# Forming weight sums and differences in a prologue by adding transfers instead of by VectorE

## The chip, the cores and the metric

The kernel runs on one core of a Trainium2 chip. The metric is the time of one execution on the device in microseconds (us); lower is better. Where several runs are given, the median counts.

## What is computed

One hybrid decoder layer on x (1024 positions x 1024 channels, float32):

```python
h = rmsnorm(x, pre_g)
proj = h @ w_in                  # 9248 columns: z, xBC, dt, q, k, v, f, z_att, g_ssm, g_att
A = ssd(silu(conv(xBC)), softplus(dt + dt_bias)) ...   # gated, group-normed
B = forgetting_attention(q, k, v, log_sigmoid(f + fgate_b)) * silu(z_att)
merged = sigmoid(g_ssm) * (A @ w_branch_ssm) + sigmoid(g_att) * (B @ w_branch_att)
out = x + rmsnorm(merged @ w_out, post_g)
```

Only the beginning matters here: h, its transpose, the first columns of h @ w_in, and dt and f (32 columns).

## The kernel before, in words

**Products with seven multiplications.** Every large product W^T h runs over blocks of 2 x 2. The weights are taken in pairs of 128 columns; one pair is four blocks a11, a12, a21, a22 (each 128 x 4 x 128, 256 KB; first digit the column group, second the half of the 1024 inputs). The transposed h is four blocks b11, b12, b21, b22 (each four tiles of 128 x 512). Instead of eight block products, seven are made, of sums of weight blocks with differences of h blocks:

- weights: S1 = a21 + a22, S2 = S1 + a11, S2 + a12, and a11 + a21
- h: T1 = b12 - b11, T2 = b22 - T1, T3 = T2 - b11, T4 = T2 - b21
- products, by the numbers that the code uses: 1 (a11, b11), 2 (a12, b21), 6 (S2, -T2), 5 (S1, T1), 7 (a11 + a21, T3), 4 (a22, T4), 3 (S2 + a12, -b22)

Each operand is kept in two parts of less precision, `h` (high) and `l` (the rest); `split` (lines 345 to 351) makes those of the weights (`wop`) with one ScalarE copy and one VectorE subtraction, `put` (line 1211) those of h (`x0h`, `x0l` for b11; x1 b21; x2 -b22; x3 T1; x4 -T2; x5 T3; x6 T4). One product ("step") is 12 matmuls of 128 x 512 on TensorE, issued as two halves of six. The results of a pair are collected in PSUM tiles `pb`, `pc`, `pd`.

**Order of the work.** `Pair` holds a pair of weight column groups; `prepare` (line 358) forms its sums and splits; `USES` (line 326) says which steps must be prepared before a raw weight buffer is free again, which is what `load_more` (line 510) goes by; raw weights have six buffers, sums two. `Stream` holds all pairs in a row and a written-out list of steps, and interleaves the first three pairs p, q, r: p1, q1, p2, q2, p6, p5, p7, p4, p3, q6, q5, q7, r1, q4, q3, then r2 and so on. `half` issues half a step; when a step begins, `ahead` (line 597) prepares the step three further on. So all the work beside the products is put between halves of steps. A scheduler then orders the instructions of each engine; `pin` keeps an instruction in its written place among the pinned ones, `tc.issue_after` puts one behind another. Each engine, and each queue that issues transfers (SyncE = SP, ScalarE = ACT, GpSimd = POOL), works strictly in its own order.

**The prologue** (from line 1166). x is loaded in eight tiles of 128 rows and normalised: tiles 0 to 3 by VectorE (line 1201), tiles 4 to 7 by GpSimd (line 1203). The first loop (k = 0 to 7) transposes tiles 0 to 3 on TensorE into PSUM (`pt`), copies them scaled to `low` (b11 and b21), splits them, and issues the halves of p1 and q1. Then `w_out` is copied within the device memory (`wo_dram`, 12 transfers of 256 KB on SyncE, line 1237), for use at the kernel's end. The second loop (j = 0 to 3, lines 1240 to 1263) transposes tiles 4 to 7: ScalarE copies the two transposed tiles out of PSUM to `up` (b12) and `b` (b22); four small products with 32 weight columns (`df`) give dt and f; VectorE forms T1 and T2 from `up`, `b`, and `low`, which are split; one half of p2 or q2 is issued; VectorE forms T3 and T4 in place of `low`. What is called the tail below are lines 1264 to 1280 and what stands right behind them: T3, T4 and -b22 are split while p6, p5, p7 and p4 run, and `dft`, with `summing`, brings dt and f into columns.

Then come convolution and state-space scan beside the further pairs, attention beside the late ones, and the final products; these the change doesn't touch.

## Time and profile before

| what | value |
|---|---|
| median of 3 runs | 1277.86 us (1277.46 to 1280.73) |
| the profiled execution's own time | 1273.87 us |
| its span, first to last instruction | 1272.2 us |
| mean granted TensorE clock | 0.999 |
| TensorE busy | 1246.1 us (98%) |
| VectorE busy | 1012.9 us (80%) |
| ScalarE busy | 794.3 us (62%) |
| GpSimd busy | 319.3 us (25%) |
| moved by transfers | 233.56 MB, 184 GB/s over the span |

How to read the profile: PE is TensorE's matrix multiply, PEld its weight load, DVE VectorE, ACT ScalarE, POOL GpSimd, SP SyncE; with a q behind it (SPq) an engine's issuing of transfers. L1203 is line 1203 of the kernel. A timeline row has start and length in us from the span's start, engine, line, operation, output <- inputs, size, and in brackets the idle time before it with what ended it; "x4" merges four such instructions in a row. A group's row has the count, the busy time in us and the mean length in ns, then the idle time before its instructions. A row of the windows view has the stretch, its length, the busy us of PE, PEld, DVE, ACT and POOL with the number of instructions, the granted clock, the busy share of the transfer engines, and GB/s.

### The profile page before, as it was taken

To read this page: it belongs to the slowest core of one execution; us is meant where nothing else is said; L and a number is where in the kernel's file an instruction comes from. 1 tells how busy PE (TensorE), PEld (TensorE's weight loads), DVE (VectorE), ACT (ScalarE), POOL (GpSimd) and SP (SyncE) were. 2 spreads that over 40 slices of the span, in tenths; PEclk is the share of its full clock that TensorE was granted. 3 is DMA by queue.
4 is the path that set the end of the run, shared out by engine and by line. 5 is a ranking of instruction groups with operands and counts; after the bars stand their busy time and mean duration, and the time that the engine had idled before them with its cause. 6 is when DMAs were issued, how large, how long until landed. Compare 5 with 4: busy or idle time off the path is not lost.

```text
span 1272.2 us, 20822 instructions
## 1 busy us (share of the span) xinstructions
PE 1246.1 (98%) x6926; PEld 982.3 (77%) x6926; DVE 1012.9 (80%) x1994; ACT 794.3 (62%) x1737; POOL 319.3 (25%) x322
## 2 busy tenths in 40 slices
PE   5999999999999999999999999999999999999997
PEld 3678888888888888888887777777777777778886
DVE  7988886988888978997767676767789767886975
ACT  7745665556665765566555666666687666844753
POOL 4000440013400241115102124223112212356062
PEclk9999999999999999999999999999999999999999
DMA  8232452545436533744447576666687657766933
GB/s 300 69 120 76 146 162 88 191 152 182 138 101 215 175 127 117 219 146 140 142 149 252 162 228 212 217 214 218 232 286 263 224 184 249 249 221 199 364 110 105
DMA packets 152236, 233.56 MB, mean 184 GB/s; under 512 B 15201, under 2 KB 60737, under 8 KB 152129
## 3 DMA queue, kind: packets, MB, share of 16 engines
q1 hardware_dynamic: 136064, 196.08, 47.7%
q10 hardware_dynamic: 10560, 18.06, 3.8%
q0 software_dynamic: 5504, 18.09, 3.7%
q8 instruction: 54, 0.88, 0.3%
q14 instruction: 54, 0.43, 0.1%
HBM read 162.99 MB, written 72.34 MB: 185 GB/s over the span
## 4 chain that ended last, share of the span: by engine, by line
PE 86%; DMA 4%; DVE 4%; ACT 4%; issue 1%; SPq 0%; POOL 0%; DVEq 0%; ACTq 0%; POOLq 0%
PE pb L128 36%; PE pc L128 21%; PE pd L128 7%; PE av L128 5%; PE pt L131 5%; PE s L128 5%; PE yps L128 2%; PE st L128 1%; ACT ex L1509 1%; DMA xt<-in_x 1%; PE tr L131 1%; PE tr_v L131 1%; DMA v<-v_dram 1%; PE df L128 1%; DVE wop L350 1%
## 5 line engine op out<-in xcount | busy, mean ns | idle before, releaser
L350 DVE TENSOR_TENSOR wop<-sum,wop 128x512 fp32r<-128x512 f32 x180 | 140.2, 780 | 53.6 <-ACT wop L349 52.6
L349 ACT ACTIVATE wop<-sum 128x512 fp32r<-128x512 f32 x180 | 112.5, 626 | 109.0 <-DVE sum L355 52.4
L1509 ACT ACTIVATE ex<-ex,nm 128x512 f32<-128x512 f32 (+1 forms) x192 | 116.2, 606 | 71.9 <-DVE nm L1505 71.6
L402 ACT ACTIVATE s<-pb 128x512 f32<-128x512 f32 x144 | 85.3, 593 | 98.2 <-PE pb L128 96.2
L128 PE MATMUL pb<-x0h,wop 128*128 128x512 f32 x384 | 131.5, 399 | 0.0
L128 PE MATMUL pb<-x6h,wop 128*128 128x512 f32 x384 | 129.5, 395 | 1.3 <-ACT s L402 1.3
L128 PE MATMUL pb<-x5h,wop 128*128 128x512 f32 x384 | 130.1, 396 | 0.7 <-ACT s L402 0.7
L350 DVE TENSOR_TENSOR wop<-raw,wop 128x512 fp32r<-128x512 f32 x144 | 105.4, 733 | 31.8 <-ACT wop L349 31.5
L128 PE MATMUL pc<-x3h,wop 128*128 128x512 f32 x384 | 129.8, 396 | 0.5 <-DVE ot L419 0.4
L128 PE MATMUL pc<-x2h,wop 128*128 128x512 f32 x384 | 130.2, 397 | 0.0
L128 PE MATMUL pb<-x4h,wop 128*128 128x512 f32 x384 | 129.1, 395 | 0.0
L1505 DVE CUSTOM_DVE_ANT_0 ex<-s,fb 128x512 f32<-128x512 f32 (+1 forms) x192 | 96.8, 552 | 20.0 <-PE s L128 14.8
L349 ACT ACTIVATE wop<-raw 128x512 fp32r<-128x512 f32 x144 | 89.7, 623 | 14.7 <-PE pd L128 6.1
L128 PE MATMUL pd<-x1h,wop 128*128 128x512 f32 x288 | 96.3, 394 | 0.0
L128 PEld LDWEIGHTS pb<-x6h,wop 128*128 128x128 f32 x384 | 72.1, 188 | 18.6 <-issue 2.0
L128 PEld LDWEIGHTS pb<-x5h,wop 128*128 128x128 f32 x384 | 72.1, 188 | 18.4 <-issue 2.0
L128 PEld LDWEIGHTS pb<-x0h,wop 128*128 128x128 f32 x384 | 72.6, 189 | 17.6 <-issue 2.9
L128 PEld LDWEIGHTS pc<-x3h,wop 128*128 128x128 f32 x384 | 72.1, 188 | 17.7 <-issue 1.5
L128 PEld LDWEIGHTS pc<-x2h,wop 128*128 128x128 f32 x384 | 72.1, 188 | 17.4 <-issue 2.4
L128 PEld LDWEIGHTS pb<-x4h,wop 128*128 128x128 f32 x384 | 72.1, 188 | 16.7 <-issue 1.9
L211 POOL TENSOR_TENSOR wd<-wd 128x256 f32<-128x256 f32 x32 | 32.4, 1011 | 205.0 <-DMA wd<-in_wo 135.0
L131 PE MATMUL pt<-ident,ex 128*128 128x128 f32 x576 | 75.1, 273 | 2.0 <-ACT ex L1509 1.4
(318 smaller groups left out, 2993.6 us busy)
## 6 DMA issues: line engine op xcount, KB each, us to landing
raw<-in_wu SPq DMA_DIRECT2D x128, 256.0 KB
csb<-cs_dram SPq DMA_DIRECT2D x32, 256.0 KB
q<-q_dram SPq DMA_DIRECT2D x32, 256.0 KB
k<-k_dram SPq DMA_DIRECT2D x16, 512.0 KB
fb<-f_dram SPq DMA_DIRECT2D x16, 512.0 KB
rb<-st_dram SPq DMA_DIRECT2D x48, 128.0 KB
wd<-in_wo SPq DMA_DIRECT2D x40, 128.0 KB
xt<-in_x SPq DMA_DIRECT2D x8, 512.0 KB
```

What stands on the lines that cost most here:

```text
L128: return tc.keep_in_program_order(nc.tensor.matmul(*args, **kw))
L131: return tc.keep_in_program_order(nc.tensor.transpose(out_, in_, idn))
L211: pin(nc.gpsimd.tensor_tensor(t[out_], t[a_], t[b_], ALU.subtract))
L349: nc.scalar.activation(op[:, 0], src, AF.Copy)
L350: nc.vector.tensor_tensor(op[:, 1], src, op[:, 0], ALU.subtract)
L402: nc.scalar.activation(s, ps, AF.Copy)
L1505: nc.vector.tensor_tensor_reduce(o, s[e][:, 0:w], fb[hp, h][:, e, 0:w], 1.0, 3.0e38, ALU.add, ALU.min, nm)
L1509: pin(nc.scalar.activation(o, o, AF.Exp, scale=-1.0, bias=nm, accum_out=hd.at(hd.sm, i, h, e)))
```

## The change

1. **Weight sums by transfers that add.** The first pair is gathered "fully", the next two "partly". `gather` loads a21 from device memory into a `sum` tile on SyncE and lets GpSimd issue a transfer that adds a22 to it: that is S1. For the first pair a second tile gets a21, then a22 and a11 added, S2. The raw a21 gets a11 added by a transfer, and S2 gets a12 added by one. For q and r S2 itself is still formed by VectorE. `FEWER` takes the place of `USES` for these pairs.
2. **When it happens.** The first pair is gathered behind the normalisation of tiles 4 to 7; each next one when step 5 of the pair before it is prepared. `ahead` prepares p6 and p5 together when p2 begins (before: p6 at the start of q1, p5 at that of p2).
3. **T1 and T2 out of PSUM.** `low` is kept negated. T1 is one VectorE instruction from the transposed tile in PSUM and `low`, T2 likewise from the other transposed tile and T1. `up` is not copied; `b22` is. The `df` products take -b11, -b21, T1 and b22, and `dft` and `summing` are adapted (signs, one more small copy).
4. **T3 and T4 by transfers that add.** T2 is added to `low` by GpSimd transfers within the on-chip memory, seven of eight; T3 of the last turn stays on VectorE. T2 has two buffers of its own.
5. **The copies of w_out** stand behind the last split of the prologue, ahead of its last five halves.

```diff
         USES = {"a11": (1, 6, 7), "a12": (2, 6), "a21": (6, 7), "a22": (6, 4)}
+        FEWER = {"a11": (1, 6), "a12": (2,), "a21": (7,), "a22": (4,)}
...
+            if self.gathers and self.s1 is not None and "a21" in names:
+                self.add(self.raw["a21"], "a11")
...
+        def add(self, t, n):
+            with tc.issue_after(self.behind) if self.behind else nullcontext():
+                nc.gpsimd.dma_start(t, self.source(n), accum_op=ALU.add)
+
+        def gather(self):
+
+            for n in range(2 if self.gathers == "fully" else 1):
+                t = wp.tile([P, KH, P], F32, tag="sum", bufs=2, name="sum")
+                nc.sync.dma_start(t, self.source("a21"))
+                self.add(t, "a22")
+                if n == 0:
+                    self.s1 = t
+                else:
+                    self.add(t, "a11")
+                    self.s2 = t
+            if "a21" in self.raw:
+                self.add(self.raw["a21"], "a11")
...
             elif which == 6:
-                self.s2 = self.total(self.s1, r["a11"])
+                if self.gathers != "fully":
+                    self.s2 = self.total(self.s1, r["a11"])
                 self.split(6, self.s2)
+                if self.gathers:
+                    self.add(self.s2, "a12")
+                    return
...
+            elif which == 7 and self.gathers:
+                self.split(7, r["a21"])
...
+            p.gathers, q.gathers, r.gathers = "fully", "partly", "partly"
...
             p.prepare(which)
+            following = self.pairs[self.pairs.index(p) + 1 :][:1]
+            if which == 5 and following and following[0].gathers:
+                following[0].gather()
             self.load_more()
...
-            if self.at + 3 < len(self.steps):
-                p, which = self.steps[self.at + 3]
+            for n in {1: (), 2: (4, 5)}.get(self.at, (self.at + 3,)):
+                if n >= len(self.steps):
+                    return
+                p, which = self.steps[n]
...
-                nc.scalar.activation(low[:, k, :], pt, AF.Copy, scale=preg[:, k : k + 1])
+                nc.scalar.activation(low[:, k, :], pt, AF.Copy, scale=less[:, k : k + 1])
...
         norm_tiles(1, tiles2)
-
-        for k, h in [(k, h) for j in range(KH) for k, h in ((j, 0), (j + KH, 0), (j + KH, 1))]:
-            pin(nc.sync.dma_start(wo_dram[k, :, half(h)], a["wo"][k * P : (k + 1) * P, half(h)]))
+        stream.pairs[0].gather()
...
-            for k in (j, j + KH):
-                pt = turned(tiles2, k)
-                up.append(b22[j] if k >= KH else pro.tile([P, HALF], F32, tag="up", bufs=1, name="up"))
-                nc.scalar.activation(up[-1], pt, AF.Copy, scale=preg[:, k : k + 1])
+            pt, pt2 = turned(tiles2, j), turned(tiles2, j + KH)
             b11, b21 = low[:, j, :], low[:, j + KH, :]
-            for n, (k, m) in enumerate(((j, b11), (j, up[0]), (j + KH, b21), (j + KH, up[1]))):
-                mm(df[32 * n : 32 * n + 32, :], wdf[:, k, :], m, start=(j == 0), stop=(j == KH - 1))
             with tc.high_priority():
                 t1 = small()
-                nc.vector.tensor_tensor(t1, up[0], b11, ALU.subtract)
+                nc.vector.scalar_tensor_tensor(t1, pt, preg[:, j : j + 1], b11, ALU.mult, ALU.add)
                 put("t1", j, t1)
-                t2 = small()
-                nc.vector.tensor_tensor(t2, up[1], t1, ALU.subtract)
+            nc.scalar.activation(b22[j], pt2, AF.Copy, scale=preg[:, j + KH : j + KH + 1])
+            steps_of(0, j, b11)
+            steps_of(2, j + KH, b21)
+            steps_of(1, j, t1)
+            steps_of(3, j + KH, b22[j])
+            with tc.high_priority():
+                t2 = pro.tile([P, HALF], F32, tag="up", bufs=2, name="t2")
+                nc.vector.scalar_tensor_tensor(t2, pt2, preg[:, j + KH : j + KH + 1], t1, ALU.mult, ALU.subtract)
                 last = put("-t2", j, t2, -1.0)
             stream.halves(1)
-            with tc.issue_after(last[1]) if j == KH - 1 else nullcontext():
-                nc.vector.tensor_tensor(b11, t2, b11, ALU.subtract)
-                nc.vector.tensor_tensor(b21, t2, b21, ALU.subtract)
+            if j < KH - 1:
+                nc.gpsimd.dma_start(b11, t2, accum_op=ALU.add)
+            else:
+                nc.vector.tensor_tensor(b11, t2, b11, ALU.add)
+            nc.gpsimd.dma_start(b21, t2, accum_op=ALU.add)
...
-        nc.scalar.activation(dft, df, AF.Identity, bias=bdf)
+        nc.scalar.activation(dft, df, AF.Identity, bias=bdf, scale=sign)
...
             put("-b22", j, b22[j], -1.0, order=pin)
+        for k, h in [(k, h) for j in range(KH) for k, h in ((j, 0), (j + KH, 0), (j + KH, 1))]:
+            pin(nc.sync.dma_start(wo_dram[k, :, half(h)], a["wo"][k * P : (k + 1) * P, half(h)]))
         stream.halves(5)
...
+        nc.vector.tensor_copy(summing[0:32, 32:64], ident[0:32, 0:32])
```

More of the change, by code (lines that the diff above doesn't have):

```diff
@@ L99, in hybrid_layer @@
     nc.vector.memset(bdf, 0.0)
-    for n in range(2):
-        nc.scalar.dma_start(bdf[32 * n : 32 * n + 32, :], a["cst"][0:32, 120:121])
+    nc.scalar.dma_start(bdf[0:32, :], a["cst"][0:32, 120:121])
     epst = const.tile([P, 1], F32, name="epst")
@@ L333, in __init__ @@
             self.s1, self.sums = None, 0
+            self.gathers = self.behind = None
         def load(self, names):
@@ L360, in prepare @@
             self.prepared.add(which)
-            if which in (5, 6) and self.s1 is None:
+            if which in (5, 6) and self.s1 is None and not self.gathers:
                 self.s1 = self.total(r["a21"], r["a22"])
@@ L516, in load_more @@
                         return
-                if not all(set(p.USES[n]) <= p.prepared for p, n in old):
+                if not all(set((p.FEWER if p.gathers else p.USES)[n]) <= p.prepared for p, n in old):
                     return
@@ L1173, in hybrid_layer @@
         nc.scalar.dma_start(preg, a["cst"][:, 80:88])
+        less = pro.tile([P, NK], F32, name="less")
+        nc.vector.tensor_scalar(less, preg, -1.0, None, ALU.mult)
+        sign = pro.tile([P, 1], F32, name="sign")
+        nc.vector.memset(sign, 1.0)
+        for n in (0, 2):
+            nc.vector.memset(sign[32 * n : 32 * n + 32, :], -1.0)
         ss = pro.tile([P, NT], F32, name="ss")
@@ L1202, in norm_tiles @@
                 else:
-                    nc.gpsimd.tensor_scalar(xt, xt, rstd[:, t : t + 1], None, ALU.mult)
+                    last = nc.gpsimd.tensor_scalar(xt, xt, rstd[:, t : t + 1], None, ALU.mult)
+            return last.ins if hf else None
         def turned(tiles, k):
@@ L1218, in put, with steps_of @@
             return [op.ins for op in made]
+        def steps_of(n, k, m):
+            j = k % KH
+            mm(df[32 * n : 32 * n + 32, :], wdf[:, k, :], m, start=(j == 0), stop=(j == KH - 1))
         tiles = load_tiles(0)
```

7 lines of the change are left out of this document (4 added, 3 removed).

## The prediction

> **What bounds the kernel now.** I read the busy shares first, then the windows view cut at the borders of the prologue's stages, then TensorE's timeline in them. The first line is the page's; in the others, after a stretch and its length, stand busy us of each engine.
>
> ```profile
> PE 1246.1 (98%) x6926; PEld 982.3 (77%) x6926; DVE 1012.9 (80%) x1994; ACT 794.3 (62%) x1737; POOL 319.3 (25%) x322
> 8.50:12.80 4.30, 1.44 (x4) 0.59 (x4) 4.14 (x8) 2.35 (x6) 0.00 (x0) 1.00 1.02 409
> 12.80:27.10 14.30, 12.36 (x56) 9.73 (x56) 12.30 (x20) 14.27 (x31) 12.89 (x4) 1.00 0.98 349
> 27.10:45.40 18.30, 18.17 (x85) 9.39 (x86) 16.80 (x28) 12.94 (x21) 0.00 (x0) 1.00 0.14 45
> 45.40:60.10 14.70, 12.56 (x57) 9.54 (x55) 14.48 (x28) 12.32 (x24) 0.93 (x2) 1.00 0.21 76
> 60.10:140.00 79.90, 79.90 (x372) 64.90 (x371) 70.24 (x134) 43.94 (x84) 4.53 (x2) 1.00 0.33 101
> ```
>
> TensorE is busy 98% of the span, and from 60.1 to 140 us all 79.90 us. So time taken off VectorE there buys nothing. What the change can win lies before 60 us, where four stages follow each other: the start, the first loop (to 27.1; ScalarE full, 14.27 of 14.30, beside a GpSimd that works 12.89), the second loop (to 45.4), and the tail of the prologue (to 60.1; VectorE full, 14.48 of 14.70, TensorE idle 14.70 - 12.56 = 2.1 us).
>
> TensorE's timeline (start, length) gives each turn of the second loop and the waits of the tail:
>
> ```profile
> 27.14 0.76 PE L131 MATMUL pt<-ident,xt 128*128 128x128 f32 x5 [0.60 <-POOL xt L1203]
> 32.02 1.03 PE L131 MATMUL pt<-ident,xt 128*128 128x128 f32 x8
> 34.03 1.04 PE L128 MATMUL df<-b,wdf 128*32 128x512 f32 x2
> 35.01 0.50 PE L128 MATMUL pd<-x1h,wop 128*128 128x512 f32 x1
> 36.49 1.03 PE L131 MATMUL pt<-ident,xt 128*128 128x128 f32 x8
> 45.42 0.40 PE L128 MATMUL pb<-x4h,wop 128*128 128x512 f32 x1
> 48.17 0.50 PE L128 MATMUL pb<-x4l,wop 128*128 128x512 f32 x1 [0.30 <-DVE x4l L1217]
> 55.67 0.50 PE L128 MATMUL pb<-x6h,wop 128*128 128x512 f32 x1 [1.31 <-ACT s L402]
> 59.23 1.10 PE L128 MATMUL pt_df<-summing,dft 128*128 128x64 f32 x8 [0.53 <-DVE summing L1304]
> ```
>
> A turn lasts 36.49 - 32.02 = 4.47 us; the first one 32.02 - 27.14 = 4.88. The second loop starts when GpSimd has scaled the last tile (the 0.60 us wait). The tail's waits are 0.30, 1.31 and 0.53 us.
>
> **The change, part by part.**
>
> *The start of the second loop.* GpSimd's row and its source view, and the reciprocal that the last tile waits for:
>
> ```profile
> 14.20 12.89 POOL L1203 TENSOR_SCALAR xt<-xt,rstd 128x1024 f32<-128x1024 f32 x4 [12.83 <-DVE rstd L1199]
> L1203 POOL TENSOR_SCALAR xt<-xt,rstd x4: 2847/3104/3892, 14.2 to 24.2; 128x1024 f32<-128x1024 f32 x4
> 22.98 0.15 DVE L1199 RECIPROCAL rstd<-rstd 128x1 f32<-128x1 f32 x1
> 27.70 0.64 ACT L349 ACTIVATE wop<-sum 128x512 fp32r<-128x512 f32 x1
> ```
>
> Four tiles back to back, 14.20 to 27.09. The change leaves these four instructions and what they wait for, so I take 0. Upper gain: at the fastest 2.847 us each they would end 12.89 - 4 x 2.847 = 1.5 us earlier, but the first loop's own matmuls run until 0.60 us before, so I bound it at -1.0 (0.60, and 0.4 for a first loop that loses one split of a sum on its full ScalarE). Loss: the new adding transfers go through this same queue; see the rivals. Splitting S2 at 27.70, ahead of the first copy out of PSUM, moves into the second loop: the first turn loses about 4.88 - 4.47 = **-0.4**.
>
> The Trainium skill (SBUF — State Buffer, "Who interferes with whom") says that a VectorE instruction with two SBUF inputs contends with a GpSimd instruction that reads SBUF. The spread from 2847 to 3892 ns agrees with that without proving it; by this rule the sums taken from VectorE would bring the -1.0, by the rows alone 0. It is a rival below.
>
> *T1 and T2 out of PSUM.* ScalarE's rows of one turn:
>
> ```profile
> 32.71 0.69 ACT L1248 ACTIVATE up<-pt,preg 128x512 f32<-128x512 f32 x1 [0.85 <-PE pt L131]
> 33.30 0.68 ACT L1248 ACTIVATE b<-pt,preg 128x512 f32<-128x512 f32 x1
> ```
>
> The copy `up` goes (4 x 0.69 us of ScalarE). But the turn's chain runs over `b`: 8 transposes (32.02 to 33.05), `b` to 33.98, the last `df` product from 34.03, the pair's six matmuls from 35.01, next transposes at 36.49. `b` is kept. Without `up` it can start about when its transposes are done, 0.1 us sooner: 4 turns x 0.1 = **-0.4**. Bounds: 0, and -0.5 (0.12 each). T1 now comes before a `df` product: if VectorE is late with it the turn grows, but two of its six instructions per turn leave. Moving the adds of T3 and T4 away and the forming of sums:
>
> ```profile
> L1254 DVE TENSOR_TENSOR th<-up,low 128x512 f32<-128x512 f32 x4 | 2.7, 684 | 0.0
> L1262 DVE TENSOR_TENSOR low<-th,low 128x512 f32<-128x512 f32 x4 | 2.7, 685 | 0.0
> L1263 DVE TENSOR_TENSOR low<-th,low 128x512 f32<-128x512 f32 x4 | 2.7, 685 | 0.0
> L355 DVE TENSOR_TENSOR sum<-raw 128x512 f32<-128x512 f32 x4 | 2.7, 687 | 0.6 <-DMA raw<-in_wu 0.6
> ```
>
> T1 and T2 stay one VectorE instruction each. Of T3's and T4's eight adds seven become transfers: 7 x 0.685 = 4.8 us off VectorE. Of the pairs' sums four leave with the first pair and three with each of the next two: 10 x 0.687 = 6.9 us. Together 11.7 us less for VectorE, nearly all of it beside a TensorE that does not wait for VectorE: its waits on VectorE in the tail are 0.30 + 0.53 us.
>
> *The tail.* ScalarE runs without a gap from 46.16 until the copy that ends the 1.31 us wait:
>
> ```profile
> 46.16 0.62 ACT L1213 ACTIVATE x4h<-th 128x512 fp32r<-128x512 f32 x1
> 55.03 0.59 ACT L402 ACTIVATE s<-pb 128x512 f32<-128x512 f32 x1
> ```
>
> With two adds fewer per turn, T2 of the last turn and so this run can start some 2 x 0.685 = 1.4 us earlier, while TensorE, by the terms above, is only 0.8 us earlier; then 0.6 of the 1.31 us wait goes. I take **-0.7** (bounds 0 and -1.31). The 0.30 us wait for x4l goes for the same reason: **-0.3**. The wait for `summing` stays: one more small copy stands on that path, +0.1 at most; I take **0**.
>
> *Adding transfers.* No transfer that adds is in this trace. Nearest are GpSimd's plain stores of the same 256 KB (first row: ns min/median/max of the issue; second: us to landing):
>
> ```profile
> L1075 POOL DMA_DIRECT2D ms_dram<-th x16: 542/542/562, 978.1 to 1115.3; - x16
> DMA to landing us min/median/max: 2.4/3.6/6.1
> ```
>
> I take 0.55 us of GpSimd per issue and 3.6 us to landing, bounds 2.4 and 6.1. By the Trainium skill (DMA: Bandwidth & Descriptors, "Anatomy of one DMA — SWDGE (gpsimd) path") 2.0 us plus the bytes at 436 GB/s would make an estimate of 2.6 us; no run here shows it for an adding transfer. S2 of the first pair is a chain of two: issued after the last tile, 27.09 + 2 x 0.55 + 3.6 + 0.55 + 3.6 = 35.9 us. Its product begins at 45.42 - 0.8 = 44.6, and two splitting instructions (1.3 us) fit. T4 of the third turn (T2 no later than the next turn's start, 36.49 + 4.47 = 41.0) lands by 41.0 + 1.1 + 6.1 = 48.2, and its product comes at about 54 (55.67 less the sum below). Cost **0**; cover gone, each is late by what it overruns.
>
> *The copies of w_out.* Twelve SyncE issues leave 12.00 and go behind the prologue:
>
> ```profile
> 12.00 10.54 SPq L1237 DMA_DIRECT2D wo_dram<-in_wo  x12
> 51.76 0.33 SPq L663 DMA_DIRECT2D q_dram<-th  x1
> 53.12 0.42 SPq L1296 DMA_DIRECT2D cst<-in_cst  x1
> 61.30 8.06 SPq L342 DMA_DIRECT2D raw<-in_wu  x4
> SPq L663 <- DVE th L661: 25.8, 2, 21.5
> 62.98 0.39 PE L128 MATMUL pb<-x4h,wop 128*128 128x512 f32 x1
> ```
>
> Behind 53.54 SyncE has nothing to issue until 61.30, 7.8 us for issues that took 10.5: the next weights go out some 2.8 us later. These are the third pair's second half; its first matmul that uses them comes after the second pair's steps (from 62.98, seven more steps of 2.72 us): cover 19 us. **0**.
>
> Smaller edits (the negated scale, one 32-row load fewer, two tiny constants) fall into the start, where VectorE waits for x: 0.
>
> **Sum**: -0.4 - 0.4 - 0.7 - 0.3 = -1.8 us, of the profiled execution's 1273.87 us (span 1272.2 and 1.7 around it), giving 1272.1. The profiled execution lies 4.0 us under the median of the runs shown, 1277.86, so I forecast 1277.86 - 1.8 = **1276.1 us**. Measurement of this kernel can tell about 0.3% (3.8 us) from no change: faster is below 1274.0, slower above 1281.7.
>
> **The rivals.**
>
> *All waits close* (faster): GpSimd, less disturbed, ends 1.0 us sooner, the 1.31 us wait goes wholly, the turn gains the upper bound: -1.0 - 0.4 - 0.5 - 0.3 - 1.31 = -3.5, with 0.5 of `summing` -4.0: 1273.9. For it: VectorE is 98% busy in the tail and loses 11.7 us. Against it: ScalarE, not VectorE, ends the longest wait.
>
> *Adds between the tiles* (slower): GpSimd's queue is in order, and its last tile cannot start before 22.98 + 0.15. If the first pair's four adds are queued ahead of that tile, they start when the third tile ends (24.24): three need no other add, 24.24 + 1.65 = 25.9; the one of a11 to S2 waits until a22 (issued second, by 25.3) has landed there, 25.3 + 3.6 = 28.9, + 0.55 = 29.5; the last tile ends at 29.5 + 2.85 = 32.3 instead of 27.09: +5.2. With the other terms +3.4: 1281.3, up to +5.9 with a landing of 6.1. It decides by whether that waiting add precedes the last tile; with only the other three ahead it costs 1.65 and the sum is near 0. For it: GpSimd's last tile is ready late. Against: the source has the tiles first.
>
> *A split waits at the head of ScalarE's queue*: the splits of S2 and S1 are called in the first turn, S2 is there at 35.9. If ScalarE's order has them before the second turn's `b` (33.30), that turn waits 2.6 us, net +0.8, 1278.7; with landings of 6.1, net +5.8.
>
> *The second pair's S1 late*: SyncE stood 21.5 us, to 51.76, at a store that waited for VectorE. If the load that begins this sum is queued behind it, it issues at 52.2, beside the twelve copies. At 3.6 us for load and add it is ready at 60.0, split by 62; if the copies double both, at 67.2 and split by 69, against a need at 61.2: between 0.8 late, net -1.0, and 7.8 late, net +6.0; I take +4, nearer the upper end, since the copies have just been issued: 1281.9.
>
> **How the numbers follow.** Chances: forecast 0.40 (own range 1274.2 to 1277.9), all waits close 0.22, adds between the tiles 0.18, split at ScalarE's head 0.10, second pair late 0.10. Faster: 0.20 of the second case and 0.05 of the forecast's end, 0.25. Slower: 0.08 of the third, 0.04 of the fourth, 0.08 of the fifth, 0.20. Within 0.3%: 0.55. The range from 1272.5 to 1282.5 takes in the faster rival and the slower ones at their usual prices.
>
> **What would show it.** Second loop: `pt` from 27.1 again, turns of 4.4 us, no `up`. Tail: no wait on x4l, a wait on `s` under 0.7 us, the fourth product of the first pair (pb<-x6h) at 53.9. GpSimd: four tiles without a transfer between them. SyncE: copies from about 54 us. Wrong if `pt` starts after 28, if ScalarE waits for a landing of `sum` in the second loop, or if TensorE has gaps after 60 us.

## The result, and the profile after

The changed kernel takes 1284.91 us (median of 6 runs, 1282.48 to 1286.1); the kernel before took 1276.96 us beside it. The ratio is 1.0056, 95% interval 1.0045 to 1.0068: slower by 7.2 us by the ratio (the two medians lie 7.95 us apart), where 1.8 us of gain were forecast. The profiled execution took 1286.1 us (span 1284.4), the slowest of its six; that of before (1273.87) lies below all of its six.

First the windows view of after, at the stretches shown for before (busy us of PE, PEld, DVE, ACT, POOL, then granted clock, DMA share, GB/s):

```profile
12.80:27.10 14.30, 11.81 (x56) 8.61 (x56) 10.86 (x17) 13.80 (x29) 12.38 (x8) 1.00 0.70 224
27.10:45.40 18.30, 14.47 (x66) 7.45 (x67) 11.80 (x17) 9.58 (x16) 10.17 (x10) 0.91 0.85 186
45.40:60.10 14.70, 12.37 (x50) 8.08 (x49) 9.58 (x17) 8.66 (x17) 1.42 (x2) 0.88 1.01 252
60.10:140.00 79.90, 77.78 (x360) 62.63 (x360) 67.58 (x132) 42.57 (x79) 4.15 (x6) 1.00 0.42 117
```

VectorE is relieved as planned: 11.80 us in the second stretch where it had 16.80, 9.58 in the third where it had 14.48. But TensorE, which is what bounds the kernel, does less there too: 14.47 instead of 18.17 us. And the transfer engines, nearly idle before (0.14 and 0.21), are at 0.85 and 1.01. No engine has become the bound; something is waited for.

TensorE's timeline in after shows where:

```profile
29.94 1.33 PE L130 MATMUL pt<-ident,xt 128*128 128x128 f32 x5 [3.40 <-POOL xt L1245]
35.39 1.03 PE L130 MATMUL pt<-ident,xt 128*128 128x128 f32 x8
40.87 1.04 PE L130 MATMUL pt<-ident,xt 128*128 128x128 f32 x8
45.16 1.03 PE L130 MATMUL pt<-ident,xt 128*128 128x128 f32 x8
53.67 0.65 PE L127 MATMUL pb<-x4h,wop 128*128 128x512 f32 x1 [1.84 <-ACT x4h L1256]
54.81 0.79 PE L127 MATMUL pb<-x4l,wop 128*128 128x512 f32 x1 [0.49 <-DVE x4l L1260]
63.12 0.50 PE L127 MATMUL pb<-x6h,wop 128*128 128x512 f32 x1 [0.98 <-ACT s L432]
67.27 0.99 PE L127 MATMUL pt_df<-summing,dft 128*128 128x64 f32 x7 [1.14 <-DVE summing L1354]
```

Against the same matmuls of before (27.14, 32.02, 36.49, 55.67, 59.23) the second loop starts 2.80 us later, its second turn 3.37, its third 4.38, `pb<-x6h` 7.45 and `pt_df` 8.04 us later. From there to 140 us the lag stays: matching all matmuls of both traces by tile and order, its median is 8.05 us in every stretch. The two profiled spans differ by 12.2 us, and 8.05 of these are made before 67 us. (Most of the rest, 3.4 us, arises between 1100 and 1120 us, where the profile of `e8_copies_only`, a kernel level with before in its median, also loses 1.7 us; it is not read here.) The 8.05 us come from three places, and one instruction stands for each (GpSimd's queue first, then ScalarE, VectorE and SyncE):

```profile
14.72 5.68 POOL L1245 TENSOR_SCALAR xt<-xt,rstd 128x1024 f32<-128x1024 f32 x2 [13.36 <-DVE rstd L1241]
20.35 1.06 POOL L353 DMA_DIRECT2D raw<-in_wu  x1
21.18 3.15 POOL L1245 TENSOR_SCALAR xt<-xt,rstd 128x1024 f32<-128x1024 f32 x1
24.00 2.11 POOL L353 DMA_DIRECT2D sum<-in_wu  x2
25.14 1.85 POOL L353 DMA_DIRECT2D raw<-in_wu  x1
25.72 4.17 POOL L1245 TENSOR_SCALAR xt<-xt,rstd 128x1024 f32<-128x1024 f32 x1
...
41.35 0.87 POOL L353 DMA_DIRECT2D sum<-in_wu  x1 [3.71 <-DMA sum<-in_wu]
41.88 1.22 POOL L1307 DMA_DIRECT2D low<-t  x1
42.42 1.58 POOL L1310 DMA_DIRECT2D low<-t  x1
```

```profile
35.11 1.15 ACT L373 ACTIVATE wop<-sum 128x512 fp32r<-128x512 f32 x2 [2.66 <-DMA sum<-in_wu]
```

```profile
52.20 0.75 DVE L1302 SCALAR_TENSOR_TENSOR t<-pt,preg,th 128x512 f32<-128x512 f32 x1 [5.12 <-DMA low<-t]
```

```profile
37.48 16.73 SPq L1328 DMA_DIRECT2D wo_dram<-in_wo  x12
```

1. **The adds stand between GpSimd's tiles.** One after the second tile, three after the third (three of the first pair's four adds, and the second pair's add to its raw a21); the fourth tile starts at 25.72 where the third ends at 21.18 + 3.15 = 24.33, takes 4.17 us instead of 2.85 to 3.89, and ends at 29.89 instead of 27.09.
2. **The split of a sum waits at the head of ScalarE's queue**, 2.66 us, until that sum has landed. Behind it stand the splits and copies of the second turn.
3. **T2 of the last turn waits 5.12 us for a buffer.** T2 has two. The one it takes is read by the adding transfer that was issued at 42.42 and landed at 52.1, beside the copies of w_out (37.48 to 54.21). That add went out late, too, 3.2 us behind its T2 (39.19): GpSimd had stood 3.71 us, to 41.35, at an add to the second pair's sum whose own load had not landed.

Behind two of these waits TensorE's granted clock is low as well, which makes the 0.91 and 0.88 of the windows view: from 29.97 and from 53.86 us it is 0.50 for 3.4 us each. The first turn of the second loop takes 5.45 us here (35.39 - 29.94), where before took 4.88.

### The profile page after: what moved, and what is told of

The parts are those of the page before. It is cut to its first block, busy times and chain, and to the rows that moved or that the text cites. A ratio compares the mean times of both kernels' runs of the same rounds, so it can differ in the third digit from the quotient of the medians.

```text
span 1284.4 us, 20858 instructions
## 1 busy us (share of the span) xinstructions
PE 1248.9 (97%) x6926; PEld 983.1 (77%) x6926; DVE 1004.8 (78%) x1982; ACT 792.6 (62%) x1733; POOL 329.3 (26%) x340
## 4 chain that ended last, share of the span: by engine, by line
PE 78%; DMA 7%; DVE 7%; ACT 4%; issue 3%; POOL 1%; SPq 0%; DVEq 0%; ACTq 0%; POOLq 0%
PE pb L127 33%; PE pc L127 19%; PE pd L127 6%; PE av L127 5%; PE s L127 4%; PE pt L130 4%; PE yps L127 2%; DVE wop L374 1%; PE st L127 1%; DVE sum L379 1%; DMA raw<-in_wu 1%; DMA sum<-in_wu 1%; PE tr L130 1%; DMA low<-t 1%; ACT ex L1559 1%
## 5 line engine op out<-in xcount | busy, mean ns | idle before, releaser
L374 DVE TENSOR_TENSOR wop<-sum,wop 128x512 fp32r<-128x512 f32 x177 | 136.3, 772 | 57.2 <-ACT wop L373 56.2
L127 PE MATMUL pc<-x3l,wop 128*128 128x512 f32 x192 | 75.8, 395 | 1.7 <-DVE x3l L278 1.7
```

Of the source, the lines that this page charges most:

```text
L127: return tc.keep_in_program_order(nc.tensor.matmul(*args, **kw))
L374: nc.vector.tensor_tensor(op[:, 1], src, op[:, 0], ALU.subtract)
```

## The experiments

Three theories. **A**: three separate waits, at the places above. **B**: an adding transfer holds the transfer engines much longer than a plain one, so that they queue up wherever they are issued, and somebody waits for the last of them. **C**: TensorE's granted clock, low behind its waits, makes the loss. Every kernel was timed in five rounds against before. Before's medians beside them were 1274.85 (first four), 1275.97 (next four) and 1276.88 us (last four); the ratios are what compares.

### Moving the adds and the copies

`e1_adds_behind`, with the mechanism that the change already has:

```diff
-        norm_tiles(1, tiles2)
+        last = norm_tiles(1, tiles2)
+        for p in stream.pairs[0:2]:
+            p.behind = last
```

> The changed kernel with one edit: the adding transfers of the first two pairs are queued on GpSimd behind the last of its four tiles. Theory A (three waits: adds between the tiles +2.9 us at the second loop's start, splits that wait for a sum +1.3, T2 waiting for its buffer while the copies of w_out fill the transfer engines +3.2, and 0.6 in the tail): the second loop starts at 27.1 instead of 29.9, the wait for T2's buffer stays; 3 to 5 us above the kernel before, instead of 8. Theory B (adding transfers are slow whatever runs beside them): the same number here. Theory C (the granted clock, 0.75 to 0.9 after the waits, is the cause and not the waits): no change, 8 us above.

Measured 1279.58 us, 1.0038 (1.0025 to 1.005): 4.8 us above before, within the 3 to 5 of A and B, and not the 8 of C. GpSimd's view of it and one row of the list of waits:

```profile
14.52 12.63 POOL L1245 TENSOR_SCALAR xt<-xt,rstd 128x1024 f32<-128x1024 f32 x4 [13.16 <-DVE rstd L1241]
```

```profile
DVE t L1304 <- DMA low<-t: 3.2, 1, 3.2
```

The tiles are together again, the second loop starts in time, and by 40 us TensorE is 1.2 us ahead of before. Then T2, now of the third turn, waits 3.2 us for its buffer. The first place is real, but its price comes back in part further on: the waits don't add up.

`e2_copies_late`: the twelve copies are issued only behind the first group of the scan, from 139.6 us on.

```diff
             stream.until(by_group[g][3])
             stream.halves(4)
             if g == 0:
+                for k, h in [(k, h) for j in range(KH) for k, h in ((j, 0), (j + KH, 0), (j + KH, 1))]:
+                    pin(nc.sync.dma_start(wo_dram[k, :, half(h)], a["wo"][k * P : (k + 1) * P, half(h)]))
```

> The changed kernel with one edit: the twelve copies of w_out are issued only after the first group of pairs, some 120 us into the span. Theory A: adds to T3 and T4 land in 5 us instead of 8.8, VectorE's wait of 5.1 us for T2's buffer goes, the start stays late: 4 to 5.5 us above the kernel before. Theory B: landings of T3 and T4 stay near 9 us, the wait stays, 7 to 8 us above. Theory C: 8 us above.

Measured 1282.12 us, 1.0063 (1.0049 to 1.0077), no better than the change; the time alone would fit B and C. But without the copies beside them the adds land sooner, as A had it:

```profile
49.06 0.75 DVE L1302 SCALAR_TENSOR_TENSOR t<-pt,preg,th 128x512 f32<-128x512 f32 x1 [2.27 <-DMA low<-t]
```

T2's wait falls from 5.12 to 2.27 us, and at 60 us TensorE is 5.1 instead of 8.05 us behind (this profile, 1280.62 us, is the fastest of the five runs). But between 170 and 185 us it loses 0.7 us more, behind the late copies (the two later kernels with them 1.4 each, those without them at most 0.2), and 0.9 us at about 240 us, where most variants lose 0.3 to 1.1 us and the change none. Neither was followed to an instruction.

`e3_both`: the edits of these two together.

> Both edits: adds behind the tiles and copies late. Theory A: all three waits go, 2 us below to 1 us above the kernel before, the prediction's first sum. Theory B: 3 to 5 us above. Theory C: unchanged at 8 above.

Measured 1281.0 us, 1.0053 (1.0041 to 1.0066): 6.8 us above before, where A gave at most 1, B 3 to 5 and C 8. TensorE is 1.4 us ahead at 40 us and 3.5 behind at 64. Now the adds wait for others on GpSimd's queue, and others for them (GpSimd, ScalarE, TensorE):

```profile
48.40 0.87 POOL L353 DMA_DIRECT2D sum<-in_wu  x1 [4.75 <-DVE wop L374]
48.94 1.23 POOL L1312 DMA_DIRECT2D low<-t  x1
```

```profile
54.65 0.63 ACT L1256 ACTIVATE x6h<-low 128x512 fp32r<-128x512 f32 x1 [1.80 <-DMA low<-t]
```

```profile
58.42 0.55 PE L127 MATMUL pb<-x6h,wop 128*128 128x512 f32 x1 [3.31 <-ACT s L432]
```

The last T4 add is ready behind T2, but stands behind an add to a weight sum that waits 4.75 us for VectorE to have split that sum. It lands at 54.6, ScalarE has stood 1.8 us for it, and TensorE waits 3.31 us. With both known places mended the loss stays, at a new place: A falls as an account of the whole.

`e8_copies_only`: before, with only the copies moved to where the change writes them.

```diff
         norm_tiles(1, tiles2)
-        for k, h in [(k, h) for j in range(KH) for k, h in ((j, 0), (j + KH, 0), (j + KH, 1))]:
-            pin(nc.sync.dma_start(wo_dram[k, :, half(h)], a["wo"][k * P : (k + 1) * P, half(h)]))
...
             put("-b22", j, b22[j], -1.0, order=pin)
+        for k, h in [(k, h) for j in range(KH) for k, h in ((j, 0), (j + KH, 0), (j + KH, 1))]:
+            pin(nc.sync.dma_start(wo_dram[k, :, half(h)], a["wo"][k * P : (k + 1) * P, half(h)]))
```

> Before, with only the twelve copies of the output weights put behind the last splits of the prologue. Theory A (the copies cost nothing of themselves; they cost beside the adding transfers): ratio 0.9995 to 1.0005, with the stretch of 45 to 60 us as before. A rival (the copies take transfer engines from the weights' loads and the store of q wherever they stand late): +0.6 to +1.6 us, 1.0005 to 1.0013.

Measured 1275.73 us, 0.9999 (0.999 to 1.0009). The copies, then issued from 30.4 to 45.8 us, cost nothing alone. (Its profile is 2 us behind that of before from 1120 us on all the same: so much is scatter of single executions, and lags that late are not read here.)

### Does the adding itself cost?

`e7_plain_transfers` is `e3_both` with every adding transfer made a plain one (both T3 and T4 lines alike); it leaves out the additions, all else stands:

```diff
-                nc.gpsimd.dma_start(t, self.source(n), accum_op=ALU.add)
+                nc.gpsimd.dma_start(t, self.source(n))
...
-                nc.gpsimd.dma_start(b11, t2, accum_op=ALU.add)
+                nc.gpsimd.dma_start(b11, t2)
```

> The kernel with the adds behind the tiles and the late copies (1.0053), but every adding transfer copies instead of adding: this leaves out the additions of the sums, of T3 and of T4, all else (the transfers' number, size, order and waits) is kept. Theory B (an adding transfer holds the transfer engines for about twice as long as a plain one, and the queue of them is what is waited for): landings 2.5 to 3.5 us instead of 4.2 to 9, no wait for a T2 buffer, none of the last x6h for T4, a time 3 to 5 us below that of the kernel with adds: 1.001 to 1.003. Theory A (places alone: what stands behind what on GpSimd's queue): the same waits with plain transfers, within 1 us of the kernel with adds: 1.0045 to 1.006.

Measured 1277.13 us, 1.0007 (0.9996 to 1.0018), against 1.0053 with the adds: at these places adding costs 0.46%, 5.9 us (by the two intervals 4 to 8). The profiles show 3.1 us of it: at 64 us TensorE is 0.4 us behind before instead of 3.5. The DMA view of 26 to 50 us, with adds and then without (GpSimd's queue: packets, MB, share of the 16 engines; then its issues: count, size, median us to landing):

```profile
q0 software_dynamic: 1729, 3.15, 77.7%
...
low<-t POOLq DMA_DIRECT2D x7, 256.0 KB, 8.1
sum<-in_wu POOLq DMA_DIRECT2D x5, 256.0 KB, 5.1
```

```profile
q0 software_dynamic: 1120, 3.67, 46.5%
...
low<-t POOLq DMA_DIRECT2D x7, 256.0 KB, 3.5
sum<-in_wu POOLq DMA_DIRECT2D x5, 256.0 KB, 3.4
```

Per MB the adds hold the engines 77.7 / 3.15 = 24.7% of the stretch, the plain transfers 46.5 / 3.67 = 12.7%: twice as long. The packets show in what form. In these 24 us the adds go in packets of 2048 bytes that take 191 ns on average, the plain transfers in packets of 4096 bytes that take 197 ns (beside those of 4 bytes in both): half the size, the same time. The same seven T3 and T4 transfers land after 8.1 instead of 3.5 us. The issue is longer too (source view of the weight sums' adds, ns min/median/max):

```profile
L353 POOL DMA_DIRECT2D sum<-in_wu x8: 864/876/1197, 26.9 to 79.7; - x8
```

```profile
L353 POOL DMA_DIRECT2D sum<-in_wu x8: 536/538/770, 27.3 to 76.6; - x8
```

No T2 waits for a buffer any more. That settles B for the larger part of what `e3_both` loses, as number, size, order and waits of the transfers in the program were the same.

### Which part of the change costs?

`e4_psum_only` keeps only the third part: no gathers, T3 and T4 on VectorE, copies in the old place.

```diff
-            p.gathers, q.gathers, r.gathers = "fully", "partly", "partly"
...
-        stream.pairs[0].gather()
...
-                t2 = pro.tile([P, HALF], F32, tag="up", bufs=2, name="t2")
+                t2 = small()
...
-            if j < KH - 1:
-                nc.gpsimd.dma_start(b11, t2, accum_op=ALU.add)
-            else:
-                nc.vector.tensor_tensor(b11, t2, b11, ALU.add)
-            nc.gpsimd.dma_start(b21, t2, accum_op=ALU.add)
+                nc.vector.tensor_tensor(b11, t2, b11, ALU.add)
+                nc.vector.tensor_tensor(b21, t2, b21, ALU.add)
```

> The kernel before with one part of the change: T1 and T2 out of PSUM (negated low, df products of -b11, -b21, T1, b22); sums, T3 and T4 on VectorE, copies of w_out in the old place. By the prediction's terms 0.4 to 1.5 us below the kernel before; if T1 out of PSUM makes VectorE late, 0 to 2 us above. Theories A, B, C do not differ here.

Measured 1279.66 us, 1.0033 (1.002 to 1.0045). It was costed at a small gain and by the medians takes more than half of the loss by itself. TensorE's rows:

```profile
29.95 0.62 PE L127 MATMUL df<-th,wdf 128*32 128x512 f32 x1 [0.95 <-DVE th L1293]
44.22 0.62 PE L127 MATMUL df<-th,wdf 128*32 128x512 f32 x1 [0.94 <-DVE th L1293]
...
60.30 1.10 PE L127 MATMUL pt_df<-summing,dft 128*128 128x64 f32 x8 [0.75 <-DVE summing L1350]
```

Before, the product `df` read ScalarE's copy `up`; now it reads T1 (`th`), and TensorE stands when VectorE has other work first. This profile, 1276.24 us, is the fastest of the five runs; at 66 us TensorE is 1.5 us behind before in it, and no trace shows the rest of the 4.2 us (0.33%).

`e11_products_from_copies` is that kernel with `df` fed as before (and so without the second instruction for `summing`):

```diff
+            up = pro.tile([P, HALF], F32, tag="up", bufs=1, name="up")
+            nc.scalar.activation(up, pt, AF.Copy, scale=preg[:, j : j + 1])
...
-            steps_of(1, j, t1)
+            steps_of(1, j, up)
...
-        nc.vector.tensor_copy(summing[0:32, 32:64], ident[0:32, 0:32])
```

> The kernel with T1 and T2 out of PSUM alone (1.0033), but with the small products of the step sizes fed as before: the first from ScalarE's copy of the pt tile instead of from T1, so that the summing matrix needs no second instruction either. Theory D (T1 and T2 out of PSUM cost by making TensorE wait for T1: 1.31 us in the last turn, and by the summing matrix's second instruction 0.2 us): both go, 0.9995 to 1.001. Rival (reading PSUM from VectorE, 750 instead of 680 ns each, and the two PSUM tiles held longer, is what costs): 1.002 to 1.004, with TensorE waiting for its pt tiles.

Measured 1277.21 us, 1.0003 (0.9993 to 1.0014). No wait for T1 is left in its timeline, and T1 and T2 still come out of PSUM. So it is not reading PSUM from VectorE that costs here, but feeding `df` from T1 together with that two-instruction constant. How is only partly seen: at 66 us the two profiles are 1.5 and 1.0 us behind before, 0.5 us of the 0.30% (3.8 us) between the ratios. And `e10_no_gather_early` below feeds `df` from T1, waits 0.94 us for it once, and is level with before.

`e5_no_gather`: the third and fourth part, no weight sum by a transfer, copies in the old place.

```diff
-            p.gathers, q.gathers, r.gathers = "fully", "partly", "partly"
...
-            for n in {1: (), 2: (4, 5)}.get(self.at, (self.at + 3,)):
+            for n in (self.at + 3,):
...
-        stream.pairs[0].gather()
```

> The change without its first part: no weight sum is formed by a transfer (VectorE and ScalarE add as before), the output weights are copied where they were before; T1 and T2 out of PSUM and T3, T4 by seven adding transfers stay. Theory A (the cost is three waits, and the largest, the T2 buffer, comes from the copies of the output weights being under way beside T4's adds): the seven adds come from 32 us on, alone on GpSimd's queue, and the copies are long done; start of the second loop 0, turns 0, T2 buffer 0, the sums' adds on VectorE beside the turns +0.5: ratio 1.000 to 1.001. Theory B (each adding transfer takes the transfer engines about 1.3 us whatever else runs, and they queue up behind one another): with 7 adds instead of 15 the queue is about half: landings near 4 us, at most one wait of 1 to 2 us in the last turn, +1 to +2.5 us in all: 1.001 to 1.002. With the 1.0033 of the kernel that has T1 and T2 out of PSUM alone as the floor, B says that T3 and T4 by transfers take away its two waits for T1 and T2 behind VectorE and so come out below it.

Measured 1278.72 us, 1.0018 (1.0008 to 1.0029). Seven adds alone don't queue up: they land 4.2 us (median) after the issue and nobody waits for one. TensorE is level with before until 56 us. What it loses comes at one place (timeline, then windows of 1 us, clock third from the end):

```profile
60.47 1.97 PE L127 MATMUL pt_df<-summing,dft 128*128 128x64 f32 x8 [2.05 <-DVE summing L1352]
```

```profile
59.00:60.00 1.00, 0.00 (x0) 0.00 (x0) 1.00 (x3) 0.71 (x3) 0.07 (x1) 1.00 0.64 252
60.00:61.00 1.00, 0.53 (x3) 0.53 (x3) 0.42 (x2) 0.63 (x1) 0.00 (x0) 0.72 0.19 41
61.00:62.00 1.00, 1.00 (x6) 1.00 (x6) 0.69 (x1) 0.00 (x0) 0.00 (x0) 0.50 0.63 197
...
66.00:67.00 1.00, 1.00 (x3) 0.75 (x3) 0.69 (x1) 0.00 (x0) 0.00 (x0) 0.50 0.00 0
67.00:68.00 1.00, 1.00 (x5) 0.82 (x4) 0.42 (x1) 0.42 (x1) 0.00 (x0) 0.87 0.00 0
```

The copy that completes `summing` stands on VectorE behind two adds of weight sums; TensorE waits 2.05 us. Then its clock is 0.50 for 0.56 + 6 + 0.26 = 6.8 us.

`e10_no_gather_early` takes that wait away: `summing` with priority, its second instruction on GpSimd.

```diff
-        nc.vector.tensor_tensor(summing, ident[:, 0:64], ident[:, 64:P], ALU.add)
-        nc.vector.tensor_copy(summing[0:32, 32:64], ident[0:32, 0:32])
+        with tc.high_priority():
+            nc.vector.tensor_tensor(summing, ident[:, 0:64], ident[:, 64:P], ALU.add)
+            nc.gpsimd.tensor_copy(summing[0:32, 32:64], ident[0:32, 0:32])
```

> The kernel without sums by transfers (1.0018), with the summing matrix formed with priority and its second instruction on GpSimd instead of VectorE. Its profile had a wait of 2.2 us for the summing matrix at 58 us, and then 8 us with a granted clock of 0.55 to 0.59. Theory of waits: the wait falls to 0.7 to 1.0 us, and only this is won: 1.0005 to 1.001. Theory of waits and clock (the long wait at 58 us also brings the lower clock that follows it): the clock stays at 1.00 in 60 to 68 us, 3 to 4.5 us are won in the profile, and the ratio comes to 0.9985 to 1.0003, with less scatter than the 1276.3 to 1282.0 us of the kernel without it.

Measured 1275.56 us, 0.9993 (0.9981 to 1.0005), the fastest of all variants and level with before. Timeline and window:

```profile
58.76 1.10 PE L127 MATMUL pt_df<-summing,dft 128*128 128x64 f32 x8 [0.43 <-POOL summing L1353]
```

```profile
60.00:68.00 8.00, 8.00 (x37) 6.59 (x36) 7.05 (x14) 3.43 (x6) 0.00 (x0) 1.00 0.51 166
```

1.62 us less wait, and the clock stays at 1.00. In the two profiles TensorE is 4.9 us earlier at 66 us, about the 5.0 us that 1.6 us of wait and half of 6.8 us at half clock make: in them C holds as a multiplier of waits. The ratio falls by 0.0025, 3.2 us; its intervals leave room for 1 to 5 us, so the medians don't tell wait and clock apart. How often the lower clock comes in unprofiled runs isn't seen.

`e6_no_t34`: the first and third part, T3 and T4 on VectorE, copies in the old place.

```diff
-            if j < KH - 1:
-                nc.gpsimd.dma_start(b11, t2, accum_op=ALU.add)
...
-            nc.gpsimd.dma_start(b21, t2, accum_op=ALU.add)
+                nc.vector.tensor_tensor(b11, t2, b11, ALU.add)
+                nc.vector.tensor_tensor(b21, t2, b21, ALU.add)
```

> The change without its second part: T3 and T4 are formed by VectorE as before, the output weights are copied where they were before; the weight sums by eight adding transfers, in their place between GpSimd's tiles, and T1 and T2 out of PSUM stay. Theory A: the second loop starts 2.9 us late and the splits wait 1.3 us, as in the change; no wait for a T2 buffer; VectorE has T3 and T4 back: +4.5 to +5.5 us at 60 us, ratio 1.0035 to 1.0045. Theory B (transfers queue up behind one another): the sums alone are at most 5 in a row, landings 4 to 5 us, the same +4 us until the second turn and nothing behind it but VectorE's own late T1 and T2 as in the kernel with these alone (+1.3): 1.004 to 1.005.

Measured 1285.49 us, 1.0071 (1.0057 to 1.0085): with fewer adds in it no faster than the change, and outside both expectations. ScalarE and TensorE:

```profile
40.33 1.15 ACT L373 ACTIVATE wop<-sum 128x512 fp32r<-128x512 f32 x2 [6.79 <-DMA sum<-in_wu]
```

```profile
43.60 1.06 PE L127 MATMUL df<-th,wdf 128*32 128x512 f32 x1 [6.04 <-DVE th L1295]
```

Here the scheduler put three of the first four adds behind GpSimd's tiles. S2's second add waits there for its first to land and goes out at 36.23, landing at 40.30. Its splits stand at the head of ScalarE's and VectorE's queues all that time, T1 behind them, TensorE behind T1. The second place is thus a chain of two landings in front of two in-order queues, and its price is set by where the scheduler puts them.

### Mending

`e12_t2_buffers`: the change with four buffers for T2.

```diff
-                t2 = pro.tile([P, HALF], F32, tag="up", bufs=2, name="t2")
+                t2 = pro.tile([P, HALF], F32, tag="up", bufs=4, name="t2")
```

> The change with four buffers for T2 instead of two, nothing else. Theory A (the wait of 5.1 us for T2's buffer in the last turn is the third of its losses, 3.2 us at 48 us): that wait goes, 4.2 us instead of 7.4 behind at 48 us, ratio 1.003 to 1.004. Theory B (the queue of adding transfers is as long, and its end is waited for elsewhere): T3 of the second turn and the last T4 land as late, x5h or x6h waits for them, and 1 to 3 us of it come back before 60 us: 1.004 to 1.0056.

Measured 1282.28 us, 1.004 (1.0024 to 1.0055). T2 waits no more, but ScalarE and TensorE do:

```profile
53.67 1.16 ACT L1256 ACTIVATE x5h<-low 128x512 fp32r<-128x512 f32 x2 [2.00 <-DMA low<-t]
```

```profile
56.55 0.50 PE L127 MATMUL pb<-x5h,wop 128*128 128x512 f32 x1 [1.19 <-ACT s L432]
61.72 0.50 PE L127 MATMUL pb<-x6h,wop 128*128 128x512 f32 x1 [2.16 <-ACT s L432]
```

The adds land as late as ever; now T3's split waits for them. In the profile TensorE is 3.7 us behind before at 50 us, where the change is 7.8 behind; at 64 us it is 6.8 behind, the change 8.05: of 4.0 us won 1.2 are left. The time lies where both theories meet; the trace speaks for B.

`e9_mended`: `e1_adds_behind`, three buffers for T2, the last T4 on VectorE, `summing` with priority.

```diff
-                t2 = pro.tile([P, HALF], F32, tag="up", bufs=2, name="t2")
+                t2 = pro.tile([P, HALF], F32, tag="up", bufs=3, name="t2")
...
+                nc.gpsimd.dma_start(b21, t2, accum_op=ALU.add)
             else:
                 nc.vector.tensor_tensor(b11, t2, b11, ALU.add)
-            nc.gpsimd.dma_start(b21, t2, accum_op=ALU.add)
+                nc.vector.tensor_tensor(b21, t2, b21, ALU.add)
...
+        with tc.high_priority():
```

> The change with four mendings: the first two pairs' weight sums are added behind GpSimd's four tiles, T2 has three buffers instead of two, the last T4 is added by VectorE, and VectorE forms the summing matrix with priority. Theory B (adding transfers queue up one behind another, and what costs is who waits for the last of the queue): the start and the turns keep the 1.2 to 1.4 us that the kernels with the adds behind the tiles gained by 40 us; no T1 or T2 waits for a buffer; the last x6h waits for no transfer; the summing matrix is 0.5 to 0.7 us less late: between -1.4 and 0 us at 64 us, ratio 0.999 to 1.0005. Rival (the copies of the output weights beside the adds hold up the loads behind them whatever the buffers): waits of 1 to 3 us in the last turn or behind it stay, 1.0015 to 1.0035. Rival (granted clock: waits of TensorE between 53 and 60 us are followed by several us at a clock of 0.55 to 0.75, as in three of the profiles): up to 3 us on top of either, where a wait of over 1 us is left there.

Measured 1278.2 us, 1.0005 (0.9987 to 1.0022): level with before. Its adds still land late (7.8 us median for T3 and T4, 6.5 for the sums), but little waits for them: T1 once for 1.29 us, behind splits whose sum landed at 40.23. So the loss can go while the queue stays, if nobody stands behind its landings; the gain of 1.4 us that TensorE has at 40 us is spent by 44. How much each of the four mendings brings was not run.

## Why the prediction was wrong

The forecast was 1276.1 us with 1282.5 as the upper end; 1284.91 came. The sign, the size and the upper end failed. Two steps failed above all: that the start of the second loop stays as it is (0, measured +2.8 us), and that the adding transfers cost 0 because their landings are covered (they queue, and 5.9 us hang on their being adds in `e7_plain_transfers`).

- **Start of the second loop: 0 forecast, +2.8 measured.** The step "the change leaves these four instructions and what they wait for" failed: `pt` starts at 29.94, behind adds between the tiles. This was the second rival, at 0.18, argued down with "the source has the tiles first". Written order didn't decide; the scheduler moved the adds forward. Which adds would go ahead was the open point in that rival, and it came out the cheap way: the add of a11 to S2, which must wait for a landing, went out behind the last tile, at 30.82. For "only the other three ahead" the prediction had 1.65 us and a sum near 0. With the second pair's add as a fourth the last tile starts 1.4 us later than the third ends, and takes 4.17 us where it took 2.85: together 2.7 of the 2.8 us, half of it in a slower tile that the prediction had not counted.
- **"The first turn loses -0.4" and the turns -0.1 each: right, and too small.** Freed of the adds between tiles, in `e1_adds_behind`, the first turn takes 31.23 - 27.21 = 4.02 us instead of 4.88, the next 4.27 instead of 4.47.

```profile
27.21 0.77 PE L130 MATMUL pt<-ident,xt 128*128 128x128 f32 x5 [1.00 <-POOL xt L1245]
31.23 1.03 PE L130 MATMUL pt<-ident,xt 128*128 128x128 f32 x8
35.50 1.03 PE L130 MATMUL pt<-ident,xt 128*128 128x128 f32 x8
```

- **T1 ahead of a `df` product: cost 0 "but two of its six instructions per turn leave".** The prediction named the new dependence and let the relief of VectorE pay for it. Alone, with the constant for `summing`, it costs 0.33% (`e4_psum_only`, against 0.03% with copies), most of it not seen in the profile. In the change VectorE has the time, and T1 is waited for behind the late splits instead.
- **The adding transfers: "0.55 us per issue and 3.6 us to landing, bounds 2.4 and 6.1".** This term decided most. Measured: 0.86 us and more of issue, 4.2 us to landing when seven come alone, 5.1 to 9.0 us (medians) in a queue. Each transfer was costed as if it were alone, by a plain store's row; the fourteen between 20 and 54 us were never added up. By the 1.55 us that one adding transfer takes of all 16 engines (77.7% of 24 us for twelve of 256 KB), they fill some 22 us. Plain, such transfers fill 46.5% of the engines' time from 26 to 50 us, adding 77.7%. The estimate of 2.6 us by the Trainium skill (DMA: Bandwidth & Descriptors, "Anatomy of one DMA — SWDGE (gpsimd) path") was further off: the soonest add in these profiles' prologues landed after 3.3 us.
- **The split at the head of ScalarE's queue: a rival at 0.10, and it happened**, with the sum there at 35.1 (35.9 forecast) and a wait of 2.66 us (2.6 forecast); the second to the third turn lost 1.0 us by it. `e6_no_t34` shows it at 6.8 us.
- **T2's buffers: not in the prediction at all.** The description of the change named "two buffers of its own". T2 of the last turn began at 52.20, right behind the landing, at 52.1, of the add that read its buffer.
- **The tail: -1.0 forecast, +0.5 measured.** The wait on `s` fell from 1.31 to 0.98 only, that on x4l grew from 0.30 to 0.49, that for `summing` from 0.53 to 1.14; "one more small copy, 0" took the copy's length for its cost, not its place in VectorE's queue. (And where the prediction's own working leaves 0.6 of the 1.31 us, it took 0.7.)
- **The copies: right that they cost 0 alone** (`e8_copies_only`), wrong about when: 37.48, not 54. SyncE issues them as soon as it comes to them, so they met the adds, beside which T2's wait is 5.12 instead of 2.27 us.
- **The granted clock: not in the prediction.** It was 0.50 for 3.4 us twice before 60 us in the profile of after, and never there in that of before.
- **The second pair's S1 late**: no wait of TensorE after `pt_df` in the stretch to 140 us shows it.

By the rule of the Trainium skill (SBUF — State Buffer, "Who interferes with whom"), a VectorE instruction with two SBUF inputs contends with a GpSimd instruction that reads SBUF; with the sums gone from VectorE the four tiles were to end 1.0 us sooner. In `e1_adds_behind` they take 12.63 instead of 12.89 us. But they take 12.63 us in `e4_psum_only` too, where VectorE still forms the sums, so no run here shows a gain by it.

The loss, then: at the places of `e3_both` the adds cost about 5.9 us by being adds (`e7_plain_transfers`; the change itself was not run with plain ones), and their place, the T1 dependence and the `summing` copy decide who pays, enlarged in the profiles by a half clock behind long waits. As these hide one another, the parts' own prices are not to be summed. Open: why an add's packets take as long as plain ones of twice the size, what the loss of `e4_psum_only` is beyond its waits, how often the half clock comes, and what the late copies disturb at 170 to 185 us.

## What to carry to other kernels

Work moved from an engine that has slack to transfers is no relief where TensorE didn't wait for that engine; it swaps instructions of known length for landings of 4 to 10 us in front of in-order queues. Before that, add up the transfers' time on the transfer engines over the stretch, and for each one name who stands behind its landing: a buffer, a split, an add behind it in the queue. And look where the scheduler puts an issue, not where the source has it.

## What the runs showed of the hardware

- An adding transfer of 256 KB holds the transfer engines twice as long as a plain one (24.7 against 12.7% of 24 us per MB) and takes 876 instead of 538 ns to issue. Its packets are of 2048 instead of 4096 bytes and take as long (191 and 197 ns; `e3_both` and `e7_plain_transfers`).
- The granted clock fell to 0.50 for 3.4 us at a time: in the change from 29.97 and from 53.86 us, in `e5_no_gather` twice in a row from 60.44 us (6.8 us, behind a wait of 2.05 us). In the 3.4 us ahead of these TensorE was busy 1%, 46% and 41%. `e1_adds_behind`, with waits of 1.40 and 1.23 us and no such stretch under 49% in the prologue, kept 1.00; no clean threshold comes out, as the clock of `e6_no_t34` fell behind a stretch of 59%, at 67.7 us. The Trainium skill (TensorE: Matmul & The Clock Gate, Part 1) says that half the clock follows at least one idle window of about 3.4 us, with windows that run freely. The 0.50 and the lengths agree with that, but two of the three stretches were only partly idle, so here less than an idle window was enough.
- With adds issued between GpSimd's tiles, VectorE's part of the split of b21 took up to 2.33 us, where it takes 0.68 otherwise (the tile's view of after, ns min/median/max); `e2_copies_late` and `e12_t2_buffers` show 2.33 us too. With the adds behind the tiles the longest was 1.19 us (`e3_both`), begun ahead of the first add, and 0.90 us in `e7_plain_transfers`. What it waited for isn't shown.

```profile
L1260 DVE SCALAR_TENSOR_TENSOR x1l<-low,x1h x4: 680/1076/2330, 24.3 to 28.6; 128x512 fp32r<-128x512 f32 x4
```
